# A hybrid decoder step: the next superblock's norm roots made amid the feed-forward, the last cross transposes moved behind output products, the first feed-forward pair in the dense banks

## The chip, the cores and the metric

The kernel runs on one core of one Trainium2 chip. Its engines are PE (TensorE, the matrix engine), DVE (VectorE), ACT (ScalarE), POOL (GpSimd) and SP (SyncE, whose queue issues nearly all transfers). The metric is the device time of one execution in microseconds (us); lower is better. The kernel before takes 2540.4 us, the median of three runs (2538.5, 2540.4 and 2542.72).

## The reference

One layer of a hybrid decoder (model width 1024) for a prompt of 2048 tokens and a sample group of 8 x 8 tokens with caches, all in float32. Cut to what matters:

```python
h = rmsnorm(x, g_mix)                      # x * rsqrt(mean(x*x) + eps) * g
q, k, v, u = split(h @ w_in)
x = x + concat([window_attention(q, k, v, sinks), pool_mix(u)]) @ w_out
h = rmsnorm(x, g_cross)
p = softmax(heads(h @ w_cq) @ mem_k.T / 16)
x = x + (p @ mem_v) @ w_co                 # memory of 256 tokens, 4 heads
h = rmsnorm(x, g_ffn)
x = x + square(relu(h @ w_up)) @ w_down    # hidden width 4096
y = rmsnorm(x, g_final)
```

The prompt's keys, values, pooling state and memory keys and values, and the sample group's, are outputs too.

## The kernel before

Activations lie transposed, channels on the 128 partitions and tokens in the free dimension. The tokens go through in three superblocks of two blocks each: 384 + 384 prompt tokens, 256 prompt tokens and 256 + 64 sample tokens, 384 + 384 prompt tokens. A float32 product is made of three matmuls: each operand is split into a rounded part "hi" and a rest "lo", and hi x hi, hi x lo and lo x hi are summed in PSUM (lines 112 to 114 in mm3, 352 to 354 in dense). So each weight tile of 128 x 1024 is loaded into a raw slot, copied to hi on ACT (L118) and its lo made on DVE (L119).

A prologue folds weights. Then each superblock runs: the first norm and the "in" product mixed with window attention and pooling, the "wo" product, cross attention with folded weights (A, then B), the feed-forward, and the final norm. Four facts matter here.

- PSUM is two pools of four banks: MM (mm0 to mm3), used by the dense products and the feed-forward's down products, and AUX (aux0 to aux3), used by the norms, attention and the feed-forward's up products. A bank is free again when the instruction that reads it, mostly on DVE, has run.
- There are six raw slots (f), twelve weight slots (w), ten scratch slots (t) and sixteen activation slots (act). Each is taken and given back in program order.
- An RMS norm (class Norm) has two parts. The roots: eight squares on ACT (L246 and L249, sq), seven adds on DVE (L250), one matmul with a matrix of 1/1024 (L258, kept in program order), Ln and Exp on ACT (L261, L262), and three small DVE steps (L263 to L265). And the application (apply): for each of eight chunks a product on DVE (L300), the rounded copy on ACT (L301) and the rest on DVE (L302).
- Every engine runs its instructions in one fixed order, which a scheduler makes when the program is built, from the order of the code, the generators that are interleaved by hand, and the slots. SP's queue is one such order as well.

The handover between superblocks: while the last up and down products run, norm1_sums loads the next superblock's input chunks (L543, four raw slots for each block) and makes the squares; its inner function rest makes the root and applies the norm. At the same time final makes the last norm's root of the finishing superblock and scales its output (L1371). L1350 adds a down product to the residual and thereby empties its MM bank.

In cross, the softmaxed probabilities of a token group of 128 are divided on POOL (L1023), transposed on PE by cross_b (four transposes, L998, the next group's scores in between) and split into hi and lo (L97, L98). The following dense product "B" reads them: its order is two chunks for block 0, two for block 1, then alternating; for each chunk of 24 matmuls the first twelve read the half hf = 0 of the probabilities and the last twelve the half hf = 1.

The feed-forward has 16 steps p. up(p) makes seven products of a Strassen-like scheme (p1 with B11, p5 with T1, p6 with T2, then with B22, T3, B21 and T4), each of 12 matmuls, in AUX banks; DVE adds (L1292) and an ACT copy (L1300) empty them. down(p) follows in MM banks. In superblock 1, where each half has 288 tokens, two up steps share a down.

Of the kernel before, what the change touches and what calls it, by code (L numbers as in the profile page):

```python
# [51 lines left out]
def kernel(ctx: ExitStack, tc: tile.TileContext, io, nW=12, nF=6, nT=10):  # L52
# [286 lines left out]
    def dense(keys, blks, hi, lo, evac, head=2, tail=3, after=None, piece=8, seq=None):  # L339
# [3 lines left out]
        for c, b in seq or order(nch, head, tail, len(blks)):  # L343
            while fetched <= c:
                loaded[fetched] = S.next(keys[fetched])
                left[fetched] = len(blks)
                fetched += 1
            th, tl = loaded[c]
            n = blks[b].n
            ps = MM.get()  # L350
            for k in range(8):
                nc.tensor.matmul(ps[:, 0:n], w8(th)[:, k, :], hi(b, k), start=k == 0, stop=False)  # L352
                nc.tensor.matmul(ps[:, 0:n], w8(th)[:, k, :], lo(b, k), start=False, stop=False)  # L353
                nc.tensor.matmul(ps[:, 0:n], w8(tl)[:, k, :], hi(b, k), start=False, stop=k == 7)  # L354
# [12 lines left out]

    later = []
# [165 lines left out]
    def norm1_sums(bl):  # L534
# [5 lines left out]
        else:  # L540
# [13 lines left out]
        return rest  # L554

# [3 lines left out]
    def superblock(s, blks, nxt):  # L559
# [430 lines left out]

        def cross():
# [43 lines left out]
            cross_b(pend)  # L1035
# [227 lines left out]
        for bl in blks:  # L1263
# [3 lines left out]
        run(dense([("B", s, c) for c in BO], pbs,  # L1267
                  lambda b, k: k4(blks[b].pt[k // 4][0], blks[b].np)[:, k % 4, :],
                  lambda b, k: k4(blks[b].pt[k // 4][1], blks[b].np)[:, k % 4, :], add_evac2, tail=2, after=after_co))
# [13 lines left out]
        def up(p, H=None):  # L1283

            def prod(w, o, nm):
                ps = AUX.get()
# [4 lines left out]
            def add(t, ps, r, free=True):  # L1291
                nc.vector.tensor_tensor(t[:, 0:hn], ps[:, 0:hn], r[:, 0:hn], ALU.add)  # L1292
                if free:
                    AUX.put(ps)
# [6 lines left out]
            AUX.put(p1)  # L1301
# [76 lines left out]
        S.resF = 0  # L1378
        Ht = [ACTS.get(), ACTS.get()]
        H = own(Ht)  # L1380
        if has:

            H1 = [t[:, 4 * PT:4 * PT + hn] for t in tt.values()][:8]
            for p in range(0, NP - 2, 2):
                up(p, H)
                up(p + 1, H1)
                down([p, p + 1], [H, H1])
        else:
            for p in range(NP - 2):
                up(p, H)  # L1390
                down([p], [H])
        up(NP - 2, H)
# [157 lines left out]
```

## Time and profile before

| | |
|---|---|
| median of the runs | 2540.4 us |
| profiled execution | 2537.34 us |
| its span | 2535.3 us |
| PE busy | 2483.3 us (98%) |
| DVE / ACT / POOL busy | 1858.8 / 1098.6 / 172.5 us |
| mean granted PE clock | 0.992 |

Times in rows are microseconds from the span's start. The stages lie at about 0 to 125 us (prologue), 125 to 960 (superblock 0), 960 to 1668 (superblock 1) and 1668 to 2535 (superblock 2). A row of the timeline gives start, length, engine, line, operation, tiles with shapes and how many alike; in brackets the idle time before it and what ended it. A row of the grouped view gives how many alike, their busy time and the mean length in ns. A row of the windows gives the window, its length, the busy time and count of PE, PE's weight loads, DVE, ACT and POOL, then the granted clock of PE, the share of DMA time and GB/s. Matmuls overlap: a row's length is longer than the distance between two starts.

### The profile page before, as it was taken

What the parts mean: (1) busy time and instruction counts of PE and PEld (TensorE: products, weight loads), DVE (VectorE), ACT (ScalarE), POOL (GpSimd) and SP (SyncE); (2) the same over time, 40 slices, a digit from 0 to 9 for tenths busy, and PEclk for the clock granted to TensorE, in tenths of its full rate; (3) what the DMA queues carried; (4) which work ended last, traced back from release to release, by engine and by line L of the source; (5) the groups of instructions that cost most, each with busy time, mean ns of one, the idle gap of its engine ahead of it and who ended that gap; (6) DMA issues with size and microseconds to landing.
All of it is one profiled execution on the core that took longest, in us unless ns stands there. A gap on an engine that the chain in (4) does not pass through costs nothing.

```text
span 2535.3 us, 38897 instructions
## 1 busy us (share of the span) xinstructions
PE 2483.3 (98%) x15199; PEld 2368.2 (93%) x15199; DVE 1858.8 (73%) x3687; ACT 1098.6 (43%) x2131; POOL 172.5 (7%) x282
## 2 busy tenths in 40 slices
PE   9899999999999999999999999999999999999998
PEld 9798989999999998996899999989998999999997
DVE  8568537877777788863787877898745877777775
ACT  7666334433333344752544334457534433333332
POOL 0015010000000001411000000003301000000000
PEclk9999999999999999999999999999999999999999
DMA  8833211222222125246522222240412121222211
GB/s 289 270 122 104 92 34 59 67 67 67 67 67 67 61 81 154 82 148 237 212 92 100 76 92 92 88 143 26 142 42 68 42 67 67 67 67 68 67 58 50
DMA packets 92540, 244.73 MB, mean 97 GB/s; under 512 B 16772, under 2 KB 31556, under 8 KB 91204
## 3 DMA queue, kind: packets, MB, share of 16 engines
q1 hardware_dynamic: 92356, 242.25, 28.8%
q8 instruction: 119, 1.95, 0.3%
q14 instruction: 65, 0.53, 0.1%
HBM read 219.53 MB, written 22.69 MB: 96 GB/s over the span
## 4 chain that ended last, share of the span: by engine, by line
PE 78%; DVE 4%; ACT 1%; DMA 1%; POOL 1%; issue 0%; POOLq 0%; DVEq 0%; ACTq 0%
PE mm L112 11%; PE mm L113 11%; PE mm L114 11%; PE aux L112 9%; PE aux L113 9%; PE aux L114 9%; PE mm L352 5%; PE mm L354 5%; PE mm L353 5%; PE aux L754 1%; PE aux L785 1%; DVE x L1371 1%; PE aux L1082 0%; ACT w L118 0%; DVE t L300 0%
## 5 line engine op out<-in xcount | busy, mean ns | idle before, releaser
L118 ACT CAST w<-f 128x1024 fp32r<-128x1024 f32 x378 | 395.6, 1050 | 731.5 <-PE mm L114 366.6
L119 DVE TENSOR_TENSOR w<-f,w 128x1024 fp32r<-128x1024 f32 x378 | 460.4, 1222 | 185.6 <-PE aux L113 98.3
L113 PE MATMUL mm<-act,w 128*128 128x384 f32 (+2 forms) x1728 | 552.8, 320 | 0.0
L114 PE MATMUL mm<-act,w 128*128 128x384 f32 (+2 forms) x1728 | 550.7, 319 | 0.8 <-DVE w L119 0.8
L112 PE MATMUL mm<-act,w 128*128 128x384 f32 (+2 forms) x1728 | 537.9, 321 | 3.4 <-DVE t L459 2.2
L112 PE MATMUL aux<-act,w 128*128 128x384 f32 (+1 forms) x1344 | 432.4, 322 | 3.6 <-DVE t L264 2.7
L114 PE MATMUL aux<-act,w 128*128 128x384 f32 (+1 forms) x1344 | 432.1, 322 | 0.0
L113 PE MATMUL aux<-act,w 128*128 128x384 f32 (+1 forms) x1344 | 431.9, 321 | 0.0
L352 PE MATMUL mm<-act,w 128*128 128x384 f32 (+2 forms) x1248 | 408.7, 328 | 7.3 <-DVE x L1350 2.9
L354 PE MATMUL mm<-act,w 128*128 128x384 f32 (+2 forms) x1248 | 405.1, 325 | 3.2 <-DVE w L119 3.1
L353 PE MATMUL mm<-act,w 128*128 128x384 f32 (+2 forms) x1248 | 405.9, 325 | 1.6 <-DVE act L302 1.2
L1350 DVE TENSOR_TENSOR x<-mm,x 128x384 f32<-128x384 f32 (+3 forms) x672 | 313.8, 493 | 125.8 <-PE mm L114 124.1
L112 PEld LDWEIGHTS mm<-act,w 128*128 128x128 f32 x1728 | 322.8, 189 | 13.3 <-ACT act L1279 7.0
L113 PEld LDWEIGHTS mm<-act,w 128*128 128x128 f32 x1728 | 326.5, 189 | 5.4 <-DVE act L1280 3.8
L114 PEld LDWEIGHTS mm<-act,w 128*128 128x128 f32 x1728 | 326.1, 189 | 2.0 <-DVE w L119 1.0
L112 PEld LDWEIGHTS aux<-act,w 128*128 128x128 f32 x1344 | 252.7, 188 | 4.8 <-DVE t L264 3.2
L114 PEld LDWEIGHTS aux<-act,w 128*128 128x128 f32 x1344 | 253.4, 189 | 0.3
L113 PEld LDWEIGHTS aux<-act,w 128*128 128x128 f32 x1344 | 253.5, 189 | 0.0
L352 PEld LDWEIGHTS mm<-act,w 128*128 128x128 f32 x1248 | 238.8, 191 | 13.7 <-issue 3.9
L353 PEld LDWEIGHTS mm<-act,w 128*128 128x128 f32 x1248 | 238.7, 191 | 7.4 <-DVE act L302 2.8
L354 PEld LDWEIGHTS mm<-act,w 128*128 128x128 f32 x1248 | 238.5, 191 | 5.6 <-DVE w L119 4.9
L1292 DVE TENSOR_TENSOR t<-aux,t 128x384 f32<-128x384 f32 (+1 forms) x336 | 169.4, 517 | 24.4 <-PE aux L114 18.7
(227 smaller groups left out, 3001.2 us busy)
## 6 DMA issues: line engine op xcount, KB each, us to landing
f<-in_wup SPq DMA_DIRECT2D x96, 512.0 KB, 3.7
f<-in_wdn SPq DMA_DIRECT2D x96, 512.0 KB, 3.7
f<-in_win SPq DMA_DIRECT2D x30, 512.0 KB, 3.8
f<-a_s SPq DMA_DIRECT2D x24, 512.0 KB, 3.8
f<-b_s SPq DMA_DIRECT2D x24, 512.0 KB, 4.4
x<-in_x SPq DMA_DIRECT2D x6, 1536.0 KB, 7.4
f<-in_wco SPq DMA_DIRECT2D x16, 512.0 KB, 5.3
f<-in_cmk SPq DMA_DIRECT2D x16, 512.0 KB, 4.4
```

Of the source, the lines that this page charges most:

```text
L112: nc.tensor.matmul(ps, Wh(k), Hh(k), start=first and i == 0, stop=False)
L113: nc.tensor.matmul(ps, Wh(k), Hl(k), start=False, stop=False)
L114: nc.tensor.matmul(ps, Wl(k), Hh(k), start=False, stop=final and i == last)
L118: nc.scalar.copy(th[:], r[:, 0:1024])
L119: nc.vector.tensor_tensor(tl[:], r[:, 0:1024], f32(th[:]), ALU.subtract)
L352: nc.tensor.matmul(ps[:, 0:n], w8(th)[:, k, :], hi(b, k), start=k == 0, stop=False)
L353: nc.tensor.matmul(ps[:, 0:n], w8(th)[:, k, :], lo(b, k), start=False, stop=False)
L354: nc.tensor.matmul(ps[:, 0:n], w8(tl)[:, k, :], hi(b, k), start=False, stop=k == 7)
L754: nc.tensor.matmul(o, q[:, j, c0:c0 + P], kz[kv][hl][:, so + k0:so + 256], start=hl == 0, stop=hl == 1)
L785: nc.tensor.transpose(ps[:, P * j:P * j + P], u.Lv[:, j, P * kb:P * kb + P], ident[:])
L1292: nc.vector.tensor_tensor(t[:, 0:hn], ps[:, 0:hn], r[:, 0:hn], ALU.add)
L1350: nc.vector.tensor_tensor(x, ps[:, o:o + n], x, ALU.add)
```

## The change

Three edits. First, a new generator roots loads the next superblock's input chunks one at a time into one raw slot, makes the squares, adds and the root of each block's first norm, and keeps the root in a scratch slot; it goes one step (one load with two squares, or a root) after each down in superblock 0 and two steps after each double down in superblock 1. norm1_sums then loads the chunks again and only applies. That is 16 more loads in all. Second, in superblocks 0 and 2 the last cross_b stands behind three pieces of the B product; its pieces are 12 matmuls now, and the transposes are held behind the third piece's last matmul. Third, up(0) uses MM banks.

```diff
@@ dense @@
-                nc.tensor.matmul(ps[:, 0:n], w8(tl)[:, k, :], hi(b, k), start=False, stop=k == 7)
+                newest[0] = nc.tensor.matmul(ps[:, 0:n], w8(tl)[:, k, :], hi(b, k), start=False, stop=k == 7)
@@ norm1_sums @@
-            nm = Norm(n, lambda k: xs[k // 2][:, n * (k % 2):n * (k % 2) + n])
-        for k in range(8):
-            nm.sq(k)
+            nm = bl.norm0
+            nm.x = lambda k: xs[k // 2][:, n * (k % 2):n * (k % 2) + n]
+        if bl.s == 0:
+            for k in range(8):
+                nm.sq(k)
 
         def rest():
-            nm.fin()
+            if bl.s == 0:
+                nm.fin()
...
+    def roots(bls):
+        for bl in bls:
+            n = bl.n
+            bl.norm0 = nm = Norm(n, None)
+            for i in range(4):
+                xs = FS.get()
+                nc.sync.dma_start(xs[:, 0:2 * n], io["x"][:, bl.xo + 2 * i * n:bl.xo + 2 * (i + 1) * n])
+                nm.x = lambda k: xs[:, n * (k % 2):n * (k % 2) + n]
+                nm.sq(2 * i)
+                nm.sq(2 * i + 1)
+                FS.put(xs)
+                yield
+            nm.fin()
+            yield
@@ cross @@
-            cross_b(pend)
+            if has:
+                cross_b(pend)
+            else:
+                rest_b.append(lambda: cross_b(pend))
@@ the B product @@
-        run(dense([("B", s, c) for c in BO], pbs,
...
+        ub = dense([("B", s, c) for c in BO], pbs,
...
+                   lambda b, k: k4(blks[b].pt[k // 4][1], blks[b].np)[:, k % 4, :], add_evac2, tail=2, after=after_co, piece=4)
+        for f in rest_b:
+            for _ in range(3):
+                next(ub)
+            with tc.issue_after(newest[0].ins):
+                f()
+        run(ub)
@@ up @@
+            bank = AUX if p else MM
+
             def prod(w, o, nm):
-                ps = AUX.get()
+                ps = bank.get()
@@ the feed-forward's loop @@
+        pre = roots(nxt or ())
...
                 down([p, p + 1], [H, H1])
+                next(pre, 1)
+                next(pre, 1)
...
                 down([p], [H])
+                next(pre, 1)
```

What it does to the order of instructions at three places follows. In the changed kernel L1381 is the old L1350 and L1402 the old L1371; the trailing digits of a name without a buffer number tell slots apart.

On DVE, at the handover from superblock 0 to 1, up to the L1350 that empties the bank mm0 (mm_109; mm_112 is mm3, mm_110 is mm1) of the last down products. Before:

```order
L300 SCALAR_TENSOR_TENSOR t_105<-f_91,vec,t_102 128x320
L300 SCALAR_TENSOR_TENSOR t_106<-f_91,vec,t_102 128x320
L1371 SCALAR_TENSOR_TENSOR x_107<-x_107,vec,t_99 128x384
L302 TENSOR_TENSOR act_67<-t_105,act_64 128x320
L302 TENSOR_TENSOR act_67<-t_106,act_64 128x320
L1371 SCALAR_TENSOR_TENSOR x_107<-x_107,vec,t_99 128x384 x7
L300 SCALAR_TENSOR_TENSOR t_97<-f_92,vec,t_102 128x320
L300 SCALAR_TENSOR_TENSOR t_105<-f_92,vec,t_102 128x320
L250 TENSOR_TENSOR t_101<-t_101,t_106 128x384
L302 TENSOR_TENSOR act_67<-t_97,act_64 128x320
L302 TENSOR_TENSOR act_67<-t_105,act_64 128x320
L1350 TENSOR_TENSOR x_108<-mm_109,x_108 128x384
```

Now:

```order
L263 SCALAR_TENSOR_TENSOR t_100<-t_104 128x384
L1381 TENSOR_TENSOR x_108<-mm_112,x_108 128x384
L264 SCALAR_TENSOR_TENSOR t_100<-aux_115,t_100 128x384
L302 TENSOR_TENSOR act_68<-t_106,act_65 128x320
L265 SCALAR_TENSOR_TENSOR t_104<-t_100,t_104 128x384
L250 TENSOR_TENSOR t_103<-t_103,t_97 128x384
L1402 SCALAR_TENSOR_TENSOR x_107<-x_107,vec,t_104 128x384 x8
L1381 TENSOR_TENSOR x_108<-mm_109,x_108 128x384
L302 TENSOR_TENSOR act_68<-t_98,act_65 128x320
L1381 TENSOR_TENSOR x_108<-mm_110,x_108 128x384
```

Before, the application to the next superblock's second block stood between the two L1350 (the rows begin six root steps after the one of mm3); now it stands earlier, and between the two L1381 are two root steps, one L302, one L250 and the eight scalings of the output.

On PE, at the start of superblock 1's feed-forward, from product B22 (act11) to product T3 (act14 and act12), with buffer numbers. Before:

```order
L112 MATMUL aux3_116<-act11_74,w7_86 128x288
L113 MATMUL aux3_116<-act11_74,w7_86 128x288
L114 MATMUL aux3_116<-act11_74,w4_83 128x288
L258 MATMUL aux2_115<-t9_106,ones_125 128x320
L112 MATMUL aux2_115<-act14_77,w7_86 128x288
L113 MATMUL aux2_115<-act14_77,w7_86 128x288
```

Now:

```order
L114 MATMUL mm2_111<-act14_77,w4_83 128x288
L112 MATMUL mm2_111<-act12_75,w7_86 128x288
L258 MATMUL aux3_116<-t0_97,ones_125 128x320
L113 MATMUL mm2_111<-act12_75,w7_86 128x288
L114 MATMUL mm2_111<-act12_75,w4_83 128x288
```

T3 moved from aux2, the bank of the root matmul L258, to mm2, and the root matmul, in aux3, stands inside T3. Three matmuls further the next step's first product follows in aux2, and then B21 in mm1.

On DVE, at the handover from superblock 1 to 2, around the first weight split L119 of superblock 2. Before:

```order
L1350 TENSOR_TENSOR x_108<-mm_112,x_108 128x288
L1350 TENSOR_TENSOR x_108<-mm_110,x_108 128x288
L119 TENSOR_TENSOR w_88<-f_95,w_80 128x1024
L1350 TENSOR_TENSOR x_108<-mm_109,x_108 128x288
L263 SCALAR_TENSOR_TENSOR t_100<-t_97 128x384
L263 SCALAR_TENSOR_TENSOR t_103<-t_101 128x256
L264 SCALAR_TENSOR_TENSOR t_100<-aux_113,t_100 128x384
L264 SCALAR_TENSOR_TENSOR t_103<-aux_114,t_103 128x256
L265 SCALAR_TENSOR_TENSOR t_97<-t_100,t_97 128x384
L265 SCALAR_TENSOR_TENSOR t_101<-t_103,t_101 128x256
```

Now:

```order
L1381 TENSOR_TENSOR x_108<-mm_110,x_108 128x288
L302 TENSOR_TENSOR act_70<-t_105,act_78 128x384
L302 TENSOR_TENSOR act_70<-t_102,act_78 128x384
L250 TENSOR_TENSOR t_106<-t_106,t_103 128x320
L1381 TENSOR_TENSOR x_108<-mm_109,x_108 128x288
L1402 SCALAR_TENSOR_TENSOR x_107<-x_107,vec,t_104 128x256 x2
L250 TENSOR_TENSOR t_106<-t_106,t_99 128x320
L300 SCALAR_TENSOR_TENSOR t_98<-f_94,vec,t_100 128x384
L300 SCALAR_TENSOR_TENSOR t_97<-f_94,vec,t_100 128x384
L119 TENSOR_TENSOR w_88<-f_91,w_80 128x1024
```

Before, the split stood ahead of the root steps and of the second block's application; now it is behind the application to both blocks, but for the last two L302, and behind six scalings of the output.

More of the change, by code (lines that the diff above doesn't have):

```diff
@@ L366, in dense @@
             yield
-    later = []
+    later, newest = [], [None]
     RW = 5
@@ L1293, in add @@
                 if free:
-                    AUX.put(ps)
+                    bank.put(ps)
                 return t
@@ L1300, in up @@
             nc.scalar.copy(r1[:, 0:hn], p1[:, 0:hn])
-            AUX.put(p1)
+            bank.put(p1)
             if H is None:
```

4 lines of the change are left out of this document (2 added, 2 removed).

## The prediction

> **What bounds the kernel now.** I read the page's first row, then what the matrix engine PE waited for, then windows with the granted clock around those waits.
>
> ```profile
> PE 2483.3 (98%) x15199; PEld 2368.2 (93%) x15199; DVE 1858.8 (73%) x3687; ACT 1098.6 (43%) x2131; POOL 172.5 (7%) x282
> ```
>
> PE is the bound; only its idle time and its slow clock can be won. Nothing in the change takes a matmul away, so the whole effect lies in waits.
>
> ```profile
> PE aux L998 <- POOL cp L1023: 3.7, 4, 1.3
> ...
> PE mm L352 <- DVE x L1350: 2.9, 1, 2.9
> PE aux L112 <- DVE t L264: 2.7, 1, 2.7
> PE mm L352 <- ACT act L301: 2.4, 4, 1.2
> ...
> PE aux L112 <- ACT t L1300: 0.9, 1, 0.9
> ```
>
> These are PE's waits (us in total, times, longest) that the three edits touch: the cross transposes L998 of superblocks 0 and 2, the handover from superblock 0 to 1 (L1350), the start of superblock 1's feed-forward (L264, L1300), and the handover from 1 to 2 (L301). The next view gives PE busy, the granted clock (PEclk) and DMA by window.
>
> ```profile
> 390.00:395.00 5.00, 4.99 (x30) 4.99 (x31) 1.81 (x3) 1.51 (x3) 0.00 (x0) 1.00 0.00 0
> 569.00:600.57 31.57, 31.57 (x182) 31.14 (x181) 24.22 (x42) 9.69 (x15) 0.00 (x0) 1.00 0.20 68
> 966.00:971.50 5.50, 5.50 (x27) 5.50 (x28) 5.50 (x14) 3.67 (x8) 0.12 (x1) 0.50 0.78 133
> 1280.00:1300.00 20.00, 15.80 (x102) 14.85 (x101) 18.24 (x37) 10.94 (x19) 0.00 (x0) 0.91 0.24 79
> 1680.00:1685.00 5.00, 3.41 (x8) 1.62 (x8) 4.96 (x11) 2.44 (x4) 0.20 (x1) 0.67 0.27 90
> 1685.00:1690.00 5.00, 5.00 (x21) 5.00 (x21) 4.93 (x11) 0.00 (x0) 0.00 (x0) 0.65 0.97 307
> 1945.00:1950.00 5.00, 3.32 (x14) 3.09 (x15) 3.11 (x7) 1.51 (x3) 1.81 (x2) 0.79 0.13 52
> 1950.00:1955.00 5.00, 5.00 (x27) 5.00 (x26) 1.16 (x3) 1.03 (x2) 0.00 (x0) 0.86 0.00 0
> ```
>
> The second row is one feed-forward iteration of superblock 0: 182 matmuls of 384 columns in 31.57 us, 0.1735 us each, full clock, no idle. The others lie just behind the waits of PE, and in all but the first of them the clock is down. A window loses (1 - clock) x its length: 2.75 us behind the handover 0 to 1, 1.8 at superblock 1's feed-forward, 1.65 + 1.75 = 3.4 at the handover 1 to 2, 1.05 + 0.7 = 1.75 behind the second cross. So a wait here costs itself and then 1.7 to 3.4 us of half clock, though not always: the first row stands behind superblock 0's cross wait, just like superblock 2's, and its clock is 1.00.
>
> **The change, part by part.** All sums are against the profiled execution (2537.34 us, span 2535.3), 3.1 us below the median of the runs, 2540.4; a saving counts the same on both.
>
> *Cross transposes (superblocks 0 and 2).* PE's rows, and DVE's half of the copy behind them:
>
> ```profile
> 387.36 0.34 PE L352 MATMUL mm<-act,w 128*128 128x384 f32 x1
> 389.03 0.44 PE L998 MATMUL aux<-ident,cp 128*128 128x128 f32 x2 [1.33 <-POOL cp L1023]
> 390.01 0.44 PE L998 MATMUL aux<-ident,cp 128*128 128x128 f32 x2 [0.55 <-POOL cp L1023]
> ```
> ```profile
> 391.11 0.69 DVE L98 TENSOR_TENSOR act<-aux,act 128x512 fp32r<-128x512 f32 x1 [1.41 <-ACT act L97]
> ```
>
> The transposes should have begun at 387.53; POOL delivered the halves at 389.03 and 390.01, a loss of about 2.4 us from start to start. Now they stand behind 36 output matmuls instead of 25: 11 x 0.1735 = 1.9 us later, at 389.4. The first pair then finds its half ready, the second waits up to 0.5 us. Saved: 2.4 - 0.5 = 1.9 us, twice, and the 1.75 us of slow clock behind the second: **5.5 us**. The cover for the copy is the other 12 matmuls of this chunk (2.1 us) and the 12 of the next chunk that read the first half of the probabilities (2.1 us): the copy ended 391.8, about 1.8 us behind the transposes, so the first reader, some 4.2 us behind, doesn't wait; if ACT and DVE were busy and it came 3 us later, 0.6 us would be lost each time. If the clock drops anyway, 3.8 us are left, so 3 to 5.5.
>
> *Handover 0 to 1.* PE, then DVE:
>
> ```profile
> 962.60 0.28 PE L354 MATMUL mm<-act,w 128*128 128x256 f32 x1
> 965.75 0.55 PE L352 MATMUL mm<-act,w 128*128 128x256 f32 x1 [2.87 <-DVE x L1350]
> ```
> ```profile
> 953.81 0.56 DVE L1350 TENSOR_TENSOR x<-mm,x 128x384 f32<-128x384 f32 x1 [0.68 <-PE mm L114]
> ...
> 959.15 3.78 DVE L1371 SCALAR_TENSOR_TENSOR x<-x,vec,t 128x384 f32<-128x384 f32 x7
> ...
> 965.05 0.55 DVE L1350 TENSOR_TENSOR x<-mm,x 128x384 f32<-128x384 f32 x1
> ```
>
> PE asked for a bank at 962.7 whose L1350 began at 965.05, 11.2 us behind the L1350 before it. Between the two stood root steps of two norms, four L300, four L302, one L250 and eight L1371. In the new order, only L264, L302, L265, L250 and the eight L1371 stand there: four at about 0.45 (L250's and L302's rows are below) and eight at 0.53 (3.78 over seven), 6.0 us. So the bank is empty near 953.8 + 0.5 + 6.0 + 0.5 = 960.8 and PE, which comes at 962.3 with the two root matmuls moved away, doesn't wait. Gone are 3.05 us from start to start, 2.75 of slow clock and 0.4 of a small wait behind them: **6.2 us**. The cover is 1.5 us; if DVE is 3 us later than this, 1.5 us of wait and a 3.4 us slow stretch (1.7 us) come back: 3 to 6.5.
>
> *Superblock 1's feed-forward, first pair in the dense banks.*
>
> ```profile
> 1280.64 0.29 PE L113 MATMUL aux<-act,w 128*128 128x288 f32 x1
> 1280.77 0.29 PE L114 MATMUL aux<-act,w 128*128 128x288 f32 x1
> ...
> 1285.20 0.40 PE L112 MATMUL aux<-act,w 128*128 128x288 f32 x1 [2.71 <-DVE t L264]
> ```
> ```profile
> 1285.07 0.44 DVE L1292 TENSOR_TENSOR t<-aux,t 128x288 f32<-128x288 f32 x1
> ...
> 1285.86 1.23 DVE L119 TENSOR_TENSOR w<-f,w 128x1024 fp32r<-128x1024 f32 x1
> ```
>
> Here the product T3 had to wait until the norm's root steps left its bank. From 1280.90 to 1285.20 PE did two root matmuls (0.3 us): 4.0 us lost, 1.0 more at L1300 and 1.8 of slow clock, 6.8 in all. In the new order T3 has a bank of its own (12 x 0.13 = 1.6 us), the root matmul stands inside it, and then come the first product of the next pair (1.6 us, in the free bank aux2) and B21, to 1284.3. B21's bank is emptied by the L1292 of 1285.07, which DVE reaches no earlier: PE waits until 1285.5, 1.2 us. Behind it the weight of L119 (now a little later, near 1287.5) costs up to 0.4. So 1.6 of 6.8 stay: **4.9 us** with 0.3 for chance. If the slow clock stays and the wait is double, 1.5; at best 6.5. In superblocks 0 and 2 the same banks are emptied at least 0.8 us before their next use and nothing waited there: 0.
>
> *Handover 1 to 2.* Mean times by shape on DVE around it, and PE's first and last rows:
>
> ```profile
> L300 DVE SCALAR_TENSOR_TENSOR t<-f,vec,t 128x384 f32<-128x384 f32 x16 | 9.3, 609 | 0.0
> L302 DVE TENSOR_TENSOR act<-t,act 128x384 fp32r<-128x384 f32 x16 | 8.5, 550 | 0.0
> ...
> L1371 DVE SCALAR_TENSOR_TENSOR x<-x,vec,t 128x256 f32<-128x256 f32 x8 | 3.6, 474 | 0.0
> L1350 DVE TENSOR_TENSOR x<-mm,x 128x288 f32<-128x288 f32 x8 | 3.4, 448 | 0.0
> L250 DVE TENSOR_TENSOR t<-t,t 128x320 f32<-128x320 f32 x7 | 3.4, 483 | 0.4 <-ACT t L249 0.4
> ```
> ```profile
> 1660.71 0.29 PE L114 MATMUL mm<-act,w 128*128 128x288 f32 x1
> ...
> 1668.50 0.34 PE L352 MATMUL mm<-act,w 128*128 128x384 f32 x1
> ...
> 1695.56 0.34 PE L352 MATMUL mm<-act,w 128*128 128x384 f32 x1
> ```
>
> Back to back an instruction takes 0.08 us less than its mean. From 1668.50 to 1695.56 PE did 96 matmuls and one root: 16.8 us of work, 10.3 lost to many waits for L301 and L302 and to 3.4 us of slow clock. Those waits go, since all of both blocks' L300 and L302 now come earlier. But they come earlier by standing ahead of the first weight split (L119) of the next superblock: behind the L1350 of the bank filled at 1661.0 (1660.5 without small waits) stand six L300 (3.2), four L302 (1.9), six L250 (2.4), six L1371 (2.4), four L1350 (1.5) and three root steps (1.0, taken like the other short shapes), then the split (1.2): 1660.5 + 0.4 + 12.4 + 1.2 = 1674.5, and 1675 with half a us for ACT's part. PE arrives near 1668 and can do 8 matmuls without that weight. It then waits about 5 us, and the clock drops for 1.7 to 3.4. The other 88 matmuls and the root take 15.4: 1675 + 15.4 + 1.7 to 3.4 = 1692.1 to 1693.8 against 1695.6. **2.3 us** saved, after 0.3 for a root matmul that only moved. If DVE comes 4 us later, 2 are lost; if it comes 1 us earlier and the clock holds, 6 are won.
>
> *The moved statistics.* 16 more loads, and in ten of 14 iterations (or five of seven double ones) two or four squares on ACT and adds on DVE. By the iteration's row DVE has 7.3 and ACT 21.9 us free in 31.57, and two adds take 1.0. The price is a collision with PE's banks, not the work: between 0 and 4 us over both superblocks, nearer the first; I take **-0.4**.
>
> Sum: 5.5 + 6.2 + 4.9 + 2.3 - 0.4 = 18.5 us; 2540.4 - 18.5 = 2521.9, so **2522**.
>
> **Rivals.** (1) *The handover 1 to 2 is clean as well*: the split is not late, all of the 10.3 us but 2 go, 18.5 + 6 = 24.5, **2516**. For: it would be so if data, not the order, kept DVE waiting. Against: DVE takes its instructions in that order, and the 12.4 us are packed without idle. (2) *Superblock 1 gives a handover back*: its attention waits on loads and on POOL, which may have their own time; if the 6.2 us come back there and the feed-forward start gives half, 18.5 - 8.5 = 10, **2530**. Against: those loads start when buffers fall free, which moves along with PE. (3) *The slow clock stays though the waits go*: the clock has a beat of its own, as the two cross waits show (1.00 behind one, 0.79 and 0.86 behind the other), and small waits that remain set it off; then 2.75 + 1.8 + 1.75 = 6.3 us of the first three places are not won, 18.5 - 6.3 = 12.2, **2528**. For: such waits of 0.5 and 1.2 us remain. Against: the feed-forward rows without any wait have clock 1.00. The Trainium skill has a rule for this, in "TensorE: Matmul & The Clock Gate", Part 1: The HAM clock gate: the half clock follows at least one idle window of about 3.4 us, and the window runs free. By it none of the three waits could have slowed the clock, and removing them would win no clock; the trace disagrees, with a clock of 0.50 right behind a wait of 2.87 us, though the free-running window fits the one cross wait of two. (4) *The change doesn't do what it says*: DVE reaches the bank of the first handover late after all, and POOL's second half still stops PE with a slow clock behind it; with all the low ends, 3 + 3 + 1.5 - 2 - 4 = 1.5 is left, **2539**, no change. (5) *Slower*: the weight loads of the feed-forward. SP's queue, DVE, and the page's list of loads:
>
> ```profile
> 596.11 0.33 SPq L178 DMA_DIRECT2D f<-in_wup  x1
> ```
> ```profile
> 603.43 0.68 DVE L183 TENSOR_TENSOR f<-f 128x512 f32<-128x512 f32 x1
> ```
> ```profile
> f<-in_wup SPq DMA_DIRECT2D x96, 512.0 KB, 3.7
> ```
>
> The load of a weight's second half is issued at 596.1, lands near 599.9 and is used at 603.4: 3.5 us to spare. The new x loads take one of the same six raw slots and stand in the same SP queue. A load that lands 3.5 us later stops DVE at L183, and the L1350s behind it hold PE's four banks, worth some 4 us more. Beyond 7.5 us each of the 15 steps costs what is over; at 2 us each, 30 - 18.5 = 11.5 slower, **2552**. Against: the slot is held for one load and two squares, 3.7 + 1.0 us, under that point.
>
> **How the numbers follow.** Forecast 0.46, rival 1 0.13, rival 2 0.15, rival 3 0.08, rival 4 0.10, rival 5 0.08. The forecast's own range from its unknowns is 2516 to 2530, which holds rivals 1 to 3 too; to hold 8 in 10 whatever is off, it reaches 2 us beyond rival 1 and to rival 4: 2514 to 2540. About 0.2% (5 us) can be told from no change here. The forecast and rivals 1 to 3 are faster: 0.82; rival 4 the same: 0.10; rival 5 slower: 0.08.
>
> **What would show it.** Right: L998 waits under 0.6 us each; no L352 wait for L1350 near 960; the L264 wait gone, with one of 1 to 1.5 us for L1292 in its place; one single L354 wait for L119 of 4 to 6 us near 1657 (1670 less the 13 us saved by then) with a clock near 0.5 behind it. Wrong: new waits of PE inside the feed-forward windows, which are now at clock 1.00 and full; slow stretches of superblock 1 between its handover and its feed-forward longer than before; or the L119 wait absent.

## The result and the profile after

The changed kernel takes 2525.5 us, the median of five runs from 2518.37 to 2528.24, against 2540.4 before (five runs, 2538.5 to 2543.17). The ratio of the times is 0.9939, with a 95% interval from 0.9924 to 0.9955: faster by 0.6%. The prediction was 2522 with a range of 2514 to 2540, so it was right in sign and range and 3.5 us too low. The profiled execution took 2526.65 us, its span is 2524.6.

The line numbers have moved: L1350 is now L1381, L1371 is L1402, L998 is L1018, L1023 is L1043, L1292 is L1323, L754 is L772, L776 is L794, L785 is L803, L855 is L873, L861 is L879, L879 is L897 and L1082 is L1105. The page's first row, then PE's waits (us in total, times, longest):

```profile
PE 2479.4 (98%) x15199; PEld 2368.9 (94%) x15199; DVE 1860.2 (74%) x3687; ACT 1099.5 (44%) x2131; POOL 172.8 (7%) x282
```
```profile
PE mm L352 <- DVE x L1381: 4.0, 2, 2.4
...
PE mm L354 <- DVE w L119: 3.1, 2, 2.4
...
PE aux L803 <- POOL x L794: 1.9, 3, 1.5
...
PE aux L114 <- DVE w L119: 1.5, 1, 1.5
...
PE mm L112 <- DVE t L1323: 0.7, 1, 0.7
...
PE aux L1018 <- POOL cp L1043: 0.2, 1, 0.2
```

The 3.7 us of the cross transposes are down to 0.2, and the L264, L301 and L302 waits are gone. L1381 still stands there, but both of its waits lie at the second handover, not the first. DVE's two L1381 around the first handover's bank, then PE's waits at the second handover:

```profile
953.75 0.55 DVE L1381 TENSOR_TENSOR x<-mm,x 128x384 f32<-128x384 f32 x1
...
960.37 0.55 DVE L1381 TENSOR_TENSOR x<-mm,x 128x384 f32<-128x384 f32 x1
```
```profile
1666.33 0.41 PE L352 MATMUL mm<-act,w 128*128 128x384 f32 x1 [2.43 <-DVE x L1381]
...
1668.44 0.69 PE L352 MATMUL mm<-act,w 128*128 128x384 f32 x1 [1.52 <-DVE x L1381]
...
1671.82 0.69 PE L354 MATMUL mm<-act,w 128*128 128x384 f32 x1 [2.38 <-DVE w L119]
```

The wait of L803 has grown (it was L785's, 0.2 us), and L114's wait for L119 in an AUX bank is new. The windows of the changed kernel at the five places (same columns as before: window, length, PE, PE's weight loads, DVE, ACT, POOL, granted clock, DMA share, GB/s):

```profile
391.00:396.00 5.00, 4.84 (x29) 4.84 (x30) 2.88 (x5) 1.92 (x4) 0.11 (x1) 1.00 0.01 3
960.00:965.00 5.00, 5.00 (x44) 5.00 (x43) 5.00 (x10) 1.94 (x4) 3.59 (x4) 1.00 0.59 238
1010.00:1015.00 5.00, 5.00 (x22) 4.60 (x22) 0.49 (x1) 0.05 (x1) 0.00 (x0) 0.50 0.17 43
1280.00:1300.00 20.00, 19.26 (x142) 18.72 (x141) 19.94 (x40) 12.39 (x20) 0.00 (x0) 1.00 0.34 110
1670.00:1675.00 5.00, 3.18 (x10) 3.18 (x11) 5.00 (x8) 1.02 (x2) 0.00 (x0) 0.50 0.74 237
1940.00:1945.00 5.00, 4.93 (x30) 4.80 (x29) 2.84 (x5) 1.96 (x4) 0.14 (x1) 1.00 0.00 0
```

Clean are both cross places, the first handover and, in its clock, the feed-forward's start. Not clean is the second handover. And a new slow place stands at 1010 to 1015, in superblock 1's sample attention: PE is shown busy for all five microseconds, with half the matmuls of a full window, at clock 0.50.

To see where the time went I compared the start of the same instruction in both traces. Four of them, of before, then of after:

```profile
1010.74 0.33 PE L861 MATMUL aux<-ident,f 128*128 128x128 f32 x1 [0.40 <-POOL f L855]
...
1152.92 1.97 PE L1082 MATMUL aux<-f,f 128*32 128x256 f32 x32
...
1712.63 0.72 PE L754 MATMUL aux<-w,act 128*128 128x256 f32 x4
...
2522.11 2.20 PE L242 MATMUL aux<-t,ones 128*128 128x384 f32 x6 [0.77 <-ACT t L239]
```
```profile
1003.27 0.33 PE L879 MATMUL aux<-ident,f 128*128 128x128 f32 x1 [0.41 <-POOL f L873]
...
1151.49 1.97 PE L1105 MATMUL aux<-f,f 128*32 128x256 f32 x32
...
1705.95 0.72 PE L772 MATMUL aux<-w,act 128*128 128x256 f32 x4
...
2511.81 2.20 PE L242 MATMUL aux<-t,ones 128*128 128x384 f32 x6 [0.75 <-ACT t L239]
```

| place | after is earlier by | change on the way |
|---|---|---|
| first transposes of superblock 1's sample attention | 7.47 us | |
| first products of its cross attention | 1.43 | 6.0 given back |
| first scores of superblock 2 | 6.68 | 5.2 won |
| last root of the final norm | 10.30 | 3.6 won |

So in this execution the first part had won 7.5 us by 1003, and 6.0 of it was gone by 1151. That loss is what most of the later experiments are about.

### The profile page after: what moved, and what is told of

Its sections match the earlier page's. It is cut to its first block, busy times and chain, and to the rows that moved or that the text cites. A ratio compares the mean times of both kernels' runs of the same rounds, so it can differ in the third digit from the quotient of the medians.

```text
span 2524.6 us, 38966 instructions
## 1 busy us (share of the span) xinstructions
PE 2479.4 (98%) x15199; PEld 2368.9 (94%) x15199; DVE 1860.2 (74%) x3687; ACT 1099.5 (44%) x2131; POOL 172.8 (7%) x282
## 4 chain that ended last, share of the span: by engine, by line
PE 54%; DVE 3%; ACT 1%; DMA 1%; POOL 1%; issue 0%; POOLq 0%; DVEq 0%; ACTq 0%; SPq 0%
PE mm L112 8%; PE mm L113 8%; PE mm L114 7%; PE aux L114 5%; PE aux L113 5%; PE aux L112 5%; PE mm L354 4%; PE mm L353 4%; PE mm L352 4%; PE aux L772 1%; PE aux L803 1%; PE aux L1105 0%; DVE x L1402 0%; DVE w L119 0%; PE aux L1018 0%
## 5 line engine op out<-in xcount | busy, mean ns | idle before, releaser
L119 DVE TENSOR_TENSOR w<-f,w 128x1024 fp32r<-128x1024 f32 x378 | 460.8, 1223 | 178.8 <-PE aux L113 93.3
L113 PE MATMUL mm<-act,w 128*128 128x384 f32 (+2 forms) x1812 | 578.6, 320 | 0.0
L114 PE MATMUL mm<-act,w 128*128 128x384 f32 (+2 forms) x1812 | 576.6, 319 | 1.9 <-DVE w L119 1.9
L112 PE MATMUL mm<-act,w 128*128 128x384 f32 (+2 forms) x1812 | 563.5, 321 | 3.6 <-ACT t L246 2.3
L352 PE MATMUL mm<-act,w 128*128 128x384 f32 (+2 forms) x1248 | 408.2, 327 | 5.6 <-DVE x L1381 4.0
L354 PE MATMUL mm<-act,w 128*128 128x384 f32 (+2 forms) x1248 | 404.5, 324 | 3.3 <-DVE w L119 3.1
L114 PE MATMUL aux<-act,w 128*128 128x384 f32 (+1 forms) x1260 | 404.1, 321 | 1.5 <-DVE w L119 1.5
L112 PE MATMUL aux<-act,w 128*128 128x384 f32 (+1 forms) x1260 | 405.2, 322 | 0.0
L113 PE MATMUL aux<-act,w 128*128 128x384 f32 (+1 forms) x1260 | 404.7, 321 | 0.0
L353 PE MATMUL mm<-act,w 128*128 128x384 f32 (+2 forms) x1248 | 404.3, 324 | 0.1
L1381 DVE TENSOR_TENSOR x<-mm,x 128x384 f32<-128x384 f32 (+3 forms) x672 | 314.3, 495 | 108.7 <-PE mm L114 104.5
L112 PEld LDWEIGHTS mm<-act,w 128*128 128x128 f32 x1812 | 337.6, 188 | 13.8 <-ACT act L1308 7.5
L113 PEld LDWEIGHTS mm<-act,w 128*128 128x128 f32 x1812 | 341.3, 188 | 5.1 <-DVE act L1309 3.7
L114 PEld LDWEIGHTS mm<-act,w 128*128 128x128 f32 x1812 | 340.9, 188 | 3.3 <-DVE w L119 2.3
L352 PEld LDWEIGHTS mm<-act,w 128*128 128x128 f32 x1248 | 238.1, 191 | 9.9 <-ACT w L118 2.7
L353 PEld LDWEIGHTS mm<-act,w 128*128 128x128 f32 x1248 | 238.1, 191 | 4.9 <-issue 2.3
L354 PEld LDWEIGHTS mm<-act,w 128*128 128x128 f32 x1248 | 238.1, 191 | 4.9 <-DVE w L119 4.5
L114 PEld LDWEIGHTS aux<-act,w 128*128 128x128 f32 x1260 | 237.0, 188 | 1.9 <-DVE w L119 1.8
L113 PEld LDWEIGHTS aux<-act,w 128*128 128x128 f32 x1260 | 237.0, 188 | 0.4
L112 PEld LDWEIGHTS aux<-act,w 128*128 128x128 f32 x1260 | 236.4, 188 | 0.4
L1323 DVE TENSOR_TENSOR t<-aux,t 128x384 f32<-128x384 f32 (+1 forms) x315 | 159.2, 519 | 21.6 <-PE aux L114 15.8
```

Source lines behind the costliest of these rows:

```text
L112: nc.tensor.matmul(ps, Wh(k), Hh(k), start=first and i == 0, stop=False)
L113: nc.tensor.matmul(ps, Wh(k), Hl(k), start=False, stop=False)
L114: nc.tensor.matmul(ps, Wl(k), Hh(k), start=False, stop=final and i == last)
L119: nc.vector.tensor_tensor(tl[:], r[:, 0:1024], f32(th[:]), ALU.subtract)
L354: newest[0] = nc.tensor.matmul(ps[:, 0:n], w8(tl)[:, k, :], hi(b, k), start=False, stop=k == 7)
L1381: nc.vector.tensor_tensor(x, ps[:, o:o + n], x, ALU.add)
```

## The experiments

### One part at a time

Run e1_cross_only is the kernel before with only the cross edit:

```diff
-            cross_b(pend)
+            if has:
+                cross_b(pend)
+            else:
+                rest_b.append(lambda: cross_b(pend))
...
+        for f in rest_b:
+            for _ in range(3):
+                next(ub)
+            with tc.issue_after(newest[0].ins):
+                f()
```

> Kernel before with the second edit alone (last cross transposes behind 36 output products in superblocks 0 and 2). Theory: PE's waits for L1023 fall from 1.33 + 0.55 us to under 0.6 at each of the two places, each place 1.9 us shorter from start to start, and the half-clock stretch of 3.4 us behind the second (1.75 us lost) goes: 5.5 us in all at these places, nothing elsewhere. Rival: POOL's second half still stops PE and the clock still drops behind the second place: 1 to 3.8 us.

Measured: 2531.68 us in one run, before 2541.47 on the same chip. By the starts of the same matmuls superblock 0's cross wins 2.0 us and superblock 2's 3.5. In its windows the clock behind both is full:

```profile
390.00:395.00 5.00, 5.00 (x31) 5.00 (x30) 2.86 (x5) 1.62 (x3) 0.00 (x0) 1.00 0.02 3
...
1945.00:1950.00 5.00, 5.00 (x30) 5.00 (x31) 2.95 (x5) 1.66 (x4) 0.00 (x0) 1.00 0.00 0
```

That is 5.5 us, the term of the prediction, and the span is 5.6 us shorter than in the profile of before (2529.7 against 2535.3). The two single runs differ by 9.8 us; the rest I put down to their spread, which one run each can't show.

Run e2_bank_only has only the first feed-forward pair in the dense banks:

```diff
+            bank = AUX if p else MM
...
-                ps = AUX.get()
+                ps = bank.get()
```

> Kernel before with the third edit alone (first pair's products in MM banks). Theory: the wait of 2.71 us for L264 at superblock 1's feed-forward goes, a wait of about 0.7 to 1.2 us for the adds L1292 comes in its place, no half clock there: 4 to 5 us from start to start at this place, 0 at the start of the other two feed-forwards. Rival: the bank was not what held T3, and a wait of 2 us or more stays with the slow clock: under 2 us.

Measured: 2537.33 us in one run. The wait for L264 is gone, and in its place stands this row (L1294 is the add that empties the bank); the next window shows PE short by 1.5 us, a wait for L119 at 1308.67, as in the full change:

```profile
1287.35 0.40 PE L112 MATMUL mm<-act,w 128*128 128x288 f32 x1 [0.75 <-DVE t L1294]
```
```profile
1280.00:1300.00 20.00, 19.25 (x143) 18.85 (x142) 19.97 (x43) 13.27 (x22) 0.00 (x0) 1.00 0.22 80
1300.00:1310.00 10.00, 8.49 (x63) 8.13 (x63) 10.00 (x22) 3.42 (x8) 0.00 (x0) 1.00 0.33 105
```

The place wins 3.6 us, less than the 4.9 predicted and than the 4 to 5 expected. DVE is busy 19.97 of 20 us and 10.00 of 10: it is behind, so a wait that is taken from L264 comes back in part at the next thing DVE owes, the weight of L119.

Run e3_roots_only has only the moved roots:

```diff
+        pre = roots(nxt or ())
...
+                next(pre, 1)
```

> Kernel before with the first edit alone (norm roots amid the feed-forward). Theory: handover 0 to 1 gains 6 to 7 us, handover 1 to 2 gains 2 to 3 us with three waits of 2 us in place of many small ones, the feed-forward loses under 1 us; the slow-clock stretch in superblock 1's window attention (6.8 us in the kernel before, 17.1 us in the changed kernel) comes out at any multiple of 3.4 us between 3.4 and 17, since it hangs on a beat that runs free of the program. Rival: the stretch is 17 us whenever the stage starts earlier, so that 5 us of the handover's gain are always given back there.

Measured: 2534.71 us in one run. The first handover wins 6.5 us (predicted 6.2). The second has these rows:

```profile
1669.21 0.41 PE L352 MATMUL mm<-act,w 128*128 128x384 f32 x1 [2.43 <-DVE x L1368]
1671.28 0.44 PE L352 MATMUL mm<-act,w 128*128 128x384 f32 x1 [1.47 <-DVE x L1368]
1674.66 0.69 PE L354 MATMUL mm<-act,w 128*128 128x384 f32 x1 [2.75 <-DVE w L119]
```

It wins 2.3 us, the predicted number, but not as one wait of 5 us for L119: two waits for L1368 (the residual add that empties a bank) come first. The moved statistics cost 0.6 us in superblock 0's feed-forward and about 1 in superblock 1's, more than expected (under 1). And the slow stretch of the sample attention is 6.83 us here, the same length as before, though the stage starts earlier: the rival, that it is 17 us whenever that is so, falls.

### The second handover: the weight split earlier

Run e4_early_split is the change with the reserve of four raw slots lifted as soon as the second block's chunks have been asked for, so that the next superblock's weights are loaded and split earlier. It was run once, then timed again as e7_early_timed:

```diff
-            hook = lambda i: norm1(nxt[1], 1) if i == 5 else None
+            hook = lambda i: (norm1(nxt[1], 1), setattr(S, 'resF', 0)) if i == 5 else None
```

> Changed kernel, and the first weight splits of the next superblock may be issued as soon as the second block's chunks have been asked for, not only when they are given back (raw slots held back: 4 becomes 0 in the hook). At handover 1 to 2 DVE then has the first split 17 instructions earlier in its order. Theory that this split's place behind the application of both blocks is what the stall of 2.4 + 1.5 + 2.4 us at handover 1 to 2 and its slow clock hang on: the wait of L354 for L119 goes or falls under 0.5 us, and 3 to 6 us are won at this place. Rival: the banks are what PE waits for, since two splits now stand ahead of the L1381 that empty them: the waits for L1381 grow by what the wait for L119 loses, 0 to 1 us.

> The version of the early split of the second handover once more, timed. Theory (its gain of about 5 us at the handover from superblock 1 to 2 is the removed weight wait and half of the slow stretch, the rest of its first look is a shorter slow stretch in superblock 1): median 2517 to 2521, faster than the changed kernel by 4 to 8 us. Rival (the gain in one look was the luck of the clock): median 2523 to 2526.

Measured: 2517.13 us in the first run; then a median of 2517.18 in four (2514.23 to 2519.82) against 2539.66 for before in 15 runs on the same chip, ratio 0.991 (0.9895 to 0.9924). It beats the kernel before. Against the changed kernel the medians say 8 us, but the changed kernel's one execution on this chip (e5_after_again, below) took 2516.23, so the runs alone don't settle it; the profile of the place does. In the timed run's profile PE's waits for L1381 and L119 and the two windows around the place, where the change had stood at clock 0.50:

```profile
PE mm L352 <- DVE x L1381: 2.2, 1, 2.2
PE mm L354 <- DVE w L119: 1.7, 3, 0.8
```
```profile
1655.00:1660.00 5.00, 2.83 (x21) 2.62 (x20) 5.00 (x10) 1.01 (x3) 0.00 (x0) 1.00 0.63 201
1660.00:1665.00 5.00, 5.00 (x31) 5.00 (x30) 3.69 (x9) 2.73 (x6) 0.52 (x2) 1.00 0.90 273
```

At the place one wait is left of three, the 2.2 us for L1381 (the longest L354 wait, 0.8, lies elsewhere), and no slow stretch follows it. By the starts of the same matmuls the place is 5.6 us better than in the change. So the second handover was limited by the late split of the next weights, as the prediction said. The full clock is not the edit's doing: the first run's profile has the same single wait (2.16 us) with a stretch of 3.41 us at half clock behind it, and the place still wins 5.3 us. What the slow clock adds there isn't separated, since in the change PE waits during much of it.

### The changed kernel again

> The changed kernel once more, unaltered, for a second profile. Theory (the slow clock is decided on a free-running grid of 3.41 us slices, and a slice with too little TensorE work makes the next one slow): the starts of all slow stretches again lie whole multiples of 3.41 us apart, the grid itself lies elsewhere against the program, and the stretch in superblock 1's sample attention, 17.07 us in the first profile (1006.19 to 1023.26), comes out different, 6.83 to 13.65 us, with the waits before it the same 0.41 and 1.00 us; the span falls by about half of what the stretch loses, so 2519 to 2524 us. Rival (the change itself lengthens the stretch, through the order of the work there): 17.07 us again within one slice, span 2524 to 2526.

Measured: 2516.23 us, span 2514.1, 10.5 us less than the first profile of the very same kernel. The same four instructions:

```profile
999.04 0.33 PE L879 MATMUL aux<-ident,f 128*128 128x128 f32 x1 [0.40 <-POOL f L873]
...
1140.28 1.97 PE L1105 MATMUL aux<-f,f 128*32 128x256 f32 x32
...
1694.51 0.72 PE L772 MATMUL aux<-w,act 128*128 128x256 f32 x4
...
2501.29 2.20 PE L242 MATMUL aux<-t,ones 128*128 128x384 f32 x6 [0.78 <-ACT t L239]
```

The way from the transposes to the cross attention takes 141.2 us here, 148.2 in the first profile and 142.2 before. The waits at its start are the same (0.40 and 1.00 us), the half clock lasts 3.41 us in place of 17.07. The expectation had said 6.83 to 13.65 and a span of 2519 to 2524; both came out below it, in the direction that the theory gave but farther. The rival, that the change's own order makes the stretch long, falls.

Counted up over the whole program but for its idle end, the half clock lasted 34.1 us in the profile of before, 34.1 in the first of the change and 13.7 in this one. With half of that taken off, as an estimate (it is too much where PE waits meanwhile), the spans are 2518.2, 2507.6 and 2507.3 us. So both profiles of the change won about 11 us apart from the clock, and the clock gave nothing in the first and 10 us in the second.

What goes with the length can be read from the slices. Within each of the twelve profiles all slow stretches begin at whole multiples of 3.413 us from one another, so there is a grid of slices that doesn't follow the program. I then added up, for each slice, the columns that the matmuls starting in it move (256 for each of 128x256, 32 for each of 128x32). The first slices of after's long stretch, and two rows that show what PE did in the third:

```profile
1002.78:1006.19 3.41, 2.00 (x13) 1.19 (x13) 2.29 (x5) 1.89 (x5) 2.67 (x4) 1.00 0.00 0
1006.19:1009.60 3.41, 3.41 (x15) 2.74 (x14) 1.27 (x4) 1.19 (x5) 0.00 (x0) 0.50 0.68 225
1009.60:1013.02 3.42, 3.42 (x16) 3.19 (x16) 0.76 (x2) 0.45 (x1) 0.00 (x0) 0.50 0.24 90
...
1019.84:1023.26 3.42, 3.42 (x18) 3.42 (x17) 1.51 (x8) 0.31 (x2) 0.00 (x0) 0.50 0.18 69
```
```profile
1009.39 0.79 PE L892 MATMUL aux<-t,t 64*128 64x128 f32 x2
1010.12 3.19 PE L897 MATMUL aux<-t,f 128*128 128x32 f32 x14
```

The third slice moves one L892 of 128 columns and 14 L897 of 32, 576 columns in all, and the next is slow though PE is busy throughout. The six slices from 1002.78 on move 2048, 2560, 576, 832, 2048 and 4096 columns; the last is dense input products and ends the stretch. In the second profile the grid lay otherwise: 2560, 2592, 2144 and 4096, and only the third was followed by a slow one. Over the twelve profiles, without the first 10 and the last 20 us of each, there are 8760 slices: all 59 with less than 2304 columns were followed by half clock, all 8636 with more than 3456 by full clock, and the 65 between went either way (24 slow, 41 not).

In the stretches left out the lower bound doesn't hold: 16 slices of the first 7 us and one at the end (e4_early_split, 2502.77) had 1664 to 2176 columns and were followed by full clock. One of them, in after:

```profile
2.68:6.09 3.41, 3.41 (x18) 3.41 (x18) 0.46 (x2) 1.00 (x3) 0.00 (x0) 1.00 0.94 261
```

What they move is mostly the prologue's transposes (L439) and, at the end, the norm's sums (L242), and a column of those costs more: the six L242 of 384 columns above took 2.20 us, where six of the feed-forward's take 1.04 (0.1735 each). So columns are a stand-in, which works for the work between; what is counted exactly stays open.

### More work, or better mixed work, in the sample attention

Run e6_filled puts dense products that nobody reads between the small ones; e8_early_filled does the same to the early split:

```diff
+            def fill(m):
+                for _ in range(m):
+                    nc.tensor.matmul(fb[:, 0:192], fz[:, 0:P], fz[:], start=True, stop=True)
...
+                fill(8 if i in (0, 2) else 0)
...
+                        fill(1)
```

> The changed kernel with matrix products whose result nobody reads put into the sample attention: eight of 192 columns ahead of the first and third pair of transposes, where TensorE waits 0.41 and 1.00 us, and one ahead of each of the 32 products of 32 columns. Nothing that the kernel computes is changed. Theory (the slow clock there is set by how little TensorE streams in a slice, the small products keeping it slow): no half clock between 1003 and 1030 us, the 16 products of 32 columns at about half of their 3.62 us; the stretch of 17.07 us cost 8.5 us, the filler costs 32 x about 0.09 = 2.9 us and some 0.5 beyond the waits that it fills, so the profile there gains 4 to 6 us on the first profile of the changed kernel, and the median, whose executions have stretches of about 10 us, comes to 2521 to 2526. Rival (the slow clock answers to the waits, or to the dense work before them, and not to how much is streamed): the stretch of 7 to 17 us stays behind the 1.00 us wait, the filler is pure cost, 2528 to 2531.

> The early split with the filler products of the run before. If the filler removes the slow stretch of the sample attention: 1 to 3 us below the early split alone, 2514 to 2519, with a narrower spread, since a stretch of varying length is gone. If the filler is pure cost: 3 us above it, 2520 to 2524.

Measured: 2534.9 us (ratio 0.9983, 0.9973 to 0.9992) and 2527.5 (0.9949, 0.9937 to 0.9962): 9 us above the change's 2525.5 and 10 above the early split's 2517.18. The stretch is 17.07 us in both. The expectation failed, and so did the rival's price (3 us), but the runs did not do what they were made for. The rows of the first:

```profile
1001.86 0.47 PE L889 MATMUL aux<-ident,f 128*128 128x128 f32 x1 [2.64 <-POOL f L876]
...
1006.79 0.51 PE L884 MATMUL aux<-fz 128*128 128x192 f32 x1
1007.10 0.52 PE L908 MATMUL aux<-t,f 128*128 128x32 f32 x2
```

The edit puts one filler to two small products. The program's scheduler left only 12 of the 32 fillers amid the small products and drew the dense input products ahead of the transposes, which then waited 2.64 us (L889 is L879 here, L908 is L897). With these a slice moved 1312 columns, well under the bound found above. It tells only that this much isn't enough.

Run e9_mixed holds the order by hand: the small products in four groups of eight, and ahead of each group six input products that stood behind them anyway. e10_early_mixed adds the early split:

```diff
+                    with ExitStack() as es:
+                        if small:
+                            es.enter_context(tc.issue_after(small[-1].ins))
+                        next(ug)
+                    with tc.issue_after(newest[0].ins):
+                        for b in range(4):
+                            small.append(nc.tensor.matmul(ov[:, :, b, :], cvz[bg][:, b, kv, :], pv[:, :, b, :], start=False, stop=kv == 1 and b == 3))
```

> The changed kernel with the 32 products of 32 columns of the sample attention cut into four groups of eight products (two calls of four), and two k-tiles of the input product, six products of 256 columns that stood behind them, put ahead of each group and held there on both sides; nothing is added or left out. Theory (a count over the ten profiles so far: every slice of 3.41 us in which TensorE streamed under 2304 columns was followed by a slice at half clock, every one with over 3456 by one at full clock): a group now streams 256 columns in 0.9 us and its dense products 1536 in 0.7, which is about 3800 columns a slice, so the slow stretch in superblock 1's sample attention, 3.41 to 17.07 us so far, shrinks to 0 or 3.41 us, started by the waits of 0.41 and 1.00 us; the median falls by 2 to 5 us, 2520.5 to 2523.5. Rival (the stretch follows the waits and runs its length whatever is streamed): still 7 to 17 us there, 2524 to 2527. Second rival: the dense products are missed behind the sample attention, where the window attention's transposes and products then wait, and the time is 2526 to 2530.

> The early split of the second handover together with the mixed order of the run before. Theory: the gains lie in different places and add, 2 to 5 us below the early split's 2517.2, 2512 to 2515.5, with no slow stretch of more than 3.41 us in the sample attention. Rival as in the run before: 2516 to 2519.

Measured: 2524.77 us (ratio 0.9945, 0.993 to 0.996) and 2519.18 (0.992, 0.9907 to 0.9934), each the same as the kernel without the mixing within what runs differ, and neither as low as expected. But the stretch is gone in both profiles. In e9's slices:

```profile
1002.92:1006.34 3.42, 3.42 (x29) 3.26 (x29) 1.64 (x5) 1.34 (x3) 0.00 (x0) 1.00 0.40 123
1006.34:1009.75 3.41, 3.41 (x32) 3.41 (x31) 0.30 (x2) 0.27 (x2) 0.00 (x0) 1.00 0.44 141
1037.06:1040.47 3.41, 1.89 (x8) 1.19 (x9) 3.22 (x14) 3.17 (x11) 0.00 (x0) 1.00 0.24 76
1040.47:1043.89 3.42, 3.42 (x12) 2.27 (x12) 3.42 (x10) 2.39 (x10) 2.49 (x3) 0.50 0.12 37
```

The first two move 3712 and 3840 columns, as expected (about 3800), and the clock stays full. It is not quite a clean test, since the 1.00 us wait went as well; the 0.39 us one stayed. The time came back later: the input products were missed behind the sample attention, where the window attention waits at 1037 to 1040 (the third row, 1664 columns) and the clock falls there instead. That is the second rival of the expectation in mechanism; its price, 2526 to 2530, was a little too high. Of the 148.2 us of the first profile's way to the cross attention 145.1 are left, where the second profile of the unmixed change had 141.2.

## Why the prediction was right, and where it was not

I take each term of its sum from the starts of the same matmuls, in the first and the second profile of the change against the one of before; "alone" is the run with that edit alone. The first handover is counted to about 984 us, and superblock 1's attention from there, so its loss is a little less than the 6.0 above.

| term | predicted | first | second | alone |
|---|---|---|---|---|
| cross, superblock 0 | 1.9 | 1.9 | 2.0 | 2.0 |
| handover 0 to 1 | 6.2 | 6.7 | 6.7 | 6.5 |
| superblock 1's attention | 0 | -5.5 | 1.4 | |
| feed-forward start | 4.9 | 3.7 | 3.9 | 3.6 |
| moved statistics | -0.4 | -1.6 | -1.3 | -1.6 |
| handover 1 to 2 | 2.3 | 2.7 | 2.2 | 2.3 |
| cross, superblock 2 | 3.65 | 3.6 | 2.7 | 3.5 |

To these come, without the change's doing, slow stretches and waits ahead of and in superblock 0 that won 0.5 us and lost 1.6 in the first profile and won 3.2 in the second.

**Right**: the cross transposes, with the wait of the second pair (0.2 us, "up to 0.5") and the clock of superblock 2. The first handover: no wait for L1381 near 960, the order of DVE's work there as forecast. Its bank was emptied at 960.37 + 0.55 = 960.9, where 960.8 was forecast. The second handover in size, and its cause, the late split. The only new wait inside the feed-forwards is the one of 1.53 us for L119, at 1305 us in superblock 1's. Rivals 1, 4 and 5 did not happen.

**Mis-sized**: the feed-forward's start. The wait for the bank was put at 1.2 us and the one for L119 at up to 0.4; measured are 0.74 and 1.53, the sum of what is left 0.7 us larger, and the clock went full as expected. DVE has no slack there (19.94 of 20 us busy). And there was less to win than the 6.8 us of the sum. Two more waits of before:

```profile
1281.69 0.81 PE L258 MATMUL aux<-t,ones 128*128 128x320 f32 x2 [0.63 <-DVE t L250]
...
1294.22 0.37 PE L112 MATMUL aux<-act,w 128*128 128x288 f32 x1 [0.87 <-ACT t L1300]
```

With the 2.71 for L264 they make 4.2 us, and half of the slow stretch of 3.41 is 1.7: 5.9, less the 2.3 that stay, is the 3.6 measured. The moved statistics were put at 0.4 us, near the low end of 0 to 4; they cost 1.3 to 1.6. No single wait shows them, and what they collide with stays open. At the second handover the form was wrong: three waits of 2.43, 1.52 and 2.38 us instead of one of 5, two of them for banks. That the total still came out at 2.2 to 2.7 against 2.3 is partly luck.

**Failed**: the step that left superblock 1's attention out of the sum. Rival 2 expected that a handover gain could be given back there, by loads and POOL, and rival 3 that the slow clock "has a beat of its own". A longer slow stretch there was one of the prediction's own signs of being wrong. What came is a mix: the place of rival 2 with the mechanism of rival 3. New waits at 1049 and 1063 (1.00 and 1.47 us) are answered by a smaller one at 1081 (0.77, where 2.22 had been); the stretch of half clock is what moved, 17.07 and 3.41 us against 6.83 before, or 13.65 us more, worth half, about 6.8. In the second profile it is 3.41 in all and the attention wins 1.4. The waits that the change brings there add up to 0.5 to 1 us more than before; the rest of what this place costs or wins is mostly the clock, and that depends on how the grid falls on one program that lies near the bound there. The sum of the terms that the change sets is 17 us in the first and 16 in the second, against the 18.5 predicted; 2540.4 less 17 is 2523.4, and the last 2 us up to the median of 2525.5 I put down to executions with the long stretch; that share was not measured. The five executions' mean clocks fit: 0.992 or 0.993 in the three from 2525.5 us up, 0.995 and 0.996 in the two below. So the waits of the sum, 12.2 us by rival 3's own reckoning, were forecast well as a sum (about 11 in both profiles), but the 6.3 us of clock were no fixed gain: 0 in one execution and 10 in another. That the median lies only 3.5 us from 2522 is in part the luck of that draw.

The prediction weighed the Trainium skill, "TensorE: Matmul & The Clock Gate", Part 1: The HAM clock gate, which ties the half clock to an idle window of about 3.4 us that runs free. The free-running grid agrees with all twelve profiles. "Idle" does not: a slice in which PE is shown busy for 3.42 of 3.42 us, moving 576 columns, was followed by half clock, and no slice that was followed by half clock, before the program's end, was without matmuls. The measurement decides; with its count, the waits of 2.87 us and of 1.3 and 0.55 us could slow the clock, and whether they did fits where the grid cut them.

## What to carry to other kernels

A stretch of small matmuls (32 columns for each weight load) counts against the clock as a wait does, though PE is shown busy; look at the granted clock by slices of 3.41 us, and keep dense products between the small ones, held there by explicit order, if there are products to spare that nobody misses later; here they were missed, and it removed the stretch without winning time. Where two profiles of one kernel differ by more than the effect you look for, compare starts of the same instructions place by place before blaming the change. Where DVE is full, a wait that you remove comes back in part at the next thing DVE owes; lifting a reserve so that the next weights are split earlier was worth 5.6 us here at its place, as much as the cross edit at both of its places (5.5).

## What the runs showed of the hardware

- The half clock comes in slices of 3.413 us on a grid that the program doesn't set: all starts of slow stretches in a profile lie whole multiples apart (in the first profile of the change at 0, 37, 259, 276, 453 and 702 slices).
- What goes with a slow next slice is how few columns were streamed: under 2304 always slow, over 3456 never, between the first 10 and the last 20 us, where some 7550 fit at the rate of the feed-forward's row (384 columns in 0.1735 us). So here it turns at about 0.3 to 0.46 of the dense rate. The prologue's transposes, whose columns cost more, kept the clock full with 1664 to 2176.
- The half clock alone moves one kernel by 10 us from execution to execution (2516.23 and 2526.65 us; 13.7 and 34.1 us of it, half the difference 10.2).
- The same wait of PE slows the clock in one execution and not in the next; by the count it matters what the wait leaves of a slice. The cross wait of superblock 0 (1.33 and 0.55 us) had clock 1.00 behind it in the profile of before (3200 columns in the slice), and 0.66 in e2_bank_only (2816), which doesn't touch it.
